# A decoder trunk on one Trainium2 core: where the weight sums of a Strassen-style product are made

## The chip, the cores and the metric

The kernel runs on one core of a Trainium2 chip. The core has five engines with a queue each, worked through in order: TensorE (PE, with PEld for its weight loads), VectorE (DVE), ScalarE (ACT), GpSimd (POOL) and SyncE (SP, which here only starts DMAs). Sixteen DMA engines carry out the transfers that SP and POOL start. An instruction waits on semaphores at the head of its queue, and everything behind it in that queue waits too. The metric is the device time of one execution in microseconds; the kernel before takes 1223.98 us (median of 3 runs, 1222.15 to 1224.19).

## The reference

Two layers over 512 tokens of 1024 features in float32, each a mixer and a squared-ReLU MLP, with RMS norms around both:

```python
for i in range(DEPTH):                       # DEPTH = 2
    h = rms_norm(x, g[0])
    h = mlstm_mixer(h, ...) if i % 2 == 0 else short_conv_mixer(h, ...)
    x = x + rms_norm(h, g[1])
    h = sqrelu_mlp(rms_norm(x, g[2]), w_up[i], w_down[i])   # 1024 -> 4096 -> 1024
    x = x + rms_norm(h, g[3])
```

The order of the stages is thus: mLSTM mixer, first MLP, short convolution, second MLP.

## The kernel before, in words

**Products.** Every float32 product is three matmuls on a high and a low half (`mm3`, L115 to L117). The halves of a weight are made from a loaded raw tile of 128x1024 by `split` (L80 on ScalarE, L81 on VectorE). Raw tiles come from a pool of 7, halves and other large tiles from a pool `u` of 15.

**Quads.** The up projections of both MLPs and the input projection of the convolution are cut into blocks of 1024x512 ("quads"), and each quad is multiplied with seven block products in place of eight (classes `Seven` and `Quad`). With the four 512x256 pieces a, b, c, d of a quad, five factors need sums of pieces: f5 = a+b, f6 = a+b+d, f7 = b+d, f3 = c+f6 (the last is the factor that `run` and `run_first` call f4). A quad without ready sums loads its pieces and adds them on VectorE in `run` (L947, L954, L971, L983). A quad with ready sums (`self.pre`) loads them as they are (`summed`, L902).

**Sums in DRAM.** Twelve quads have ready sums: the first three of the first MLP (`early`), the convolution's six and the first three of the second MLP (`later`). Class `Sums` makes them with DMAs alone: stage 0 copies a, d, b, c from DRAM to four DRAM tiles, started by SyncE (L367); stages 1 to 3 add with accumulating DMAs started by GpSimd (L370): f5 += b and f7 += d, then f6 += f5, then f3 += f6. Each transfer has 512 KB. The stages of `early` stand in the code beside the mixer's `scores_and_core` and output gate, those of `later` beside the loop of the first MLP, but they depend on nothing that is computed.

**The mixer.** Its order is: values for the first two heads (`v_half` 0), gates, eight query and key blocks, values for the other heads (`v_half` 1) with `scores` and `core` in between, eight output gate blocks, then the output projection (`last_product`). GpSimd makes the causal mask for `scores` (L639, `affine_select`), the powers -1/2 in `core` (L743) and those of the norms (L173).

**The first MLP.** `enter` starts the first three quads, then `run_first` and `run` finish quads 0 and 1; then for g = 0 to 5 `down(g)` multiplies with the down weights (two halves `hf` of four token tiles `t`, the sums in `ys` by ScalarE L1053 for g = 0 and VectorE L1055 after) and `run` works on quad g + 2; `fetch_x` (L826, on GpSimd) loads the residual, and `last_product` ends the MLP with gains on GpSimd (L321).

**Order.** A scheduler puts each engine's instructions in order when the program is built; loads and copies from SyncE share one queue, accumulating DMAs and GpSimd's arithmetic another.

Of the kernel before, what the change touches and what calls it, by code (L numbers as in the profile page):

```python
# [8 lines left out]
F32 = mybir.dt.float32  # L9
# [3 lines left out]
ALU = mybir.AluOpType  # L13

P = 128
# [20 lines left out]
AHEAD = 3  # L36
# [3 lines left out]
def tile_hybrid_trunk(  # L40
# [15 lines left out]
    nc = tc.nc  # L56
# [5 lines left out]
    dram = ctx.enter_context(tc.tile_pool(name="dram", bufs=1, space=bass.MemoryType.DRAM))  # L62
# [4 lines left out]
    def pu():  # L67
        return psum("pu", 4)

    def pd():  # L70
        return psum("pd", 2)
# [21 lines left out]
    def raw_tile(shape, dtype=F32):  # L93
        return big.tile([P] + shape, dtype, tag="raw", name="raw", bufs=NRAW)
# [6 lines left out]
    def piece(src, a):  # L101
        return halved(load(src, a), a)
# [6 lines left out]
    def cols_piece(wm, c0):  # L109
        return piece(wm[:, c0 : c0 + P].rearrange("(ko p) m -> p ko m", p=P), KO)  # L110
# [75 lines left out]
    class Plain:  # L186
        def __init__(self):
            self.f = [[unit([4, S], F32R) for _ in range(2)] for _ in range(2)]
# [161 lines left out]
    class Sums:  # L350
# [3 lines left out]
        def __init__(self, wm, c0, c1):  # L354
            def src(kh, c):
                return wm[kh * 512 : (kh + 1) * 512, c : c + 256].rearrange("(p q) m -> q p m", q=P)

            self.a, self.b, self.c, self.d = src(0, c0), src(0, c1), src(1, c0), src(1, c1)
            self.f = [
                dram.tile([P, 4, 256], F32, name=f"f{n}_{len(made)}") for n in (5, 6, 7, 3)  # L360
            ]

        def stage(self, i):
            f5, f6, f7, f3 = self.f
            if i == 0:
                for f, blk in zip(self.f, (self.a, self.d, self.b, self.c)):
                    nc.sync.dma_start(f, blk)  # L367
                return
            for f, blk in (((f5, self.b), (f7, self.d)), ((f6, f5),), ((f3, f6),))[i - 1]:
                nc.gpsimd.dma_start(f, blk, accum_op=ALU.add, max_dma_last_dim=D)  # L370

    made = {}

    def sums_of(key, wm, cols):
        for c in cols:
            made[key, c[0]] = Sums(wm, *c)
        return [made[key, c[0]] for c in cols]
# [82 lines left out]
    later = tc.keep_in_program_order  # L460
# [70 lines left out]
    def rows():  # L531
# [24 lines left out]
    a = T1[0:H, :]  # L556
    nc.vector.scalar_tensor_tensor(
        out=a, in0=thi, scalar=CAP, in1=nb, op0=ALU.mult, op1=ALU.add
# [4 lines left out]
    for c in range(NT):  # L563
# [6 lines left out]
            out=mprev[:, c + 1 : c + 2], in0=M[:, last], in1=nb[:, last], op=ALU.subtract  # L570
        )

    def by_chunk(r):
        return r.rearrange("h (c l) -> h c l", l=P)
# [3 lines left out]
        out=by_chunk(T1[32 : 32 + H, :]),  # L578
        in0=mprev[:, 0:NT].unsqueeze(2).broadcast_to([H, NT, P]),
        in1=M3,  # L580
        op=ALU.subtract,
# [3 lines left out]
        out=by_chunk(T1[96 : 96 + H, :]),  # L585
        in0=by_chunk(a),
        in1=M3[:, :, P - 1 : P].broadcast_to([H, NT, P]),
        op=ALU.subtract,
# [37 lines left out]
    for h in range(H):  # L626
# [4 lines left out]
        for c in range(NT):  # L631
# [8 lines left out]
            out=DT[:, h, :, :],  # L640
# [127 lines left out]
    def take_o(j, o, late):  # L768
        sg = half_kb()
        nc.scalar.activation(sg, o, AF.Sigmoid)  # L770
        put_off(late, lambda: gated(j, sg))
# [12 lines left out]
    def up_cols(gs):  # L784
        return [(g * 512, g * 512 + 256) for g in gs]

    early = sums_of(0, w_up[0], up_cols(range(AHEAD)))
    later = sums_of(
        "conv",
        w_in_conv[0],  # L790
# [3 lines left out]
        + up_cols([1]),  # L794
    ) + sums_of(1, w_up[1], up_cols(range(AHEAD)))

    def all_of(sums, i):
        for sm in sums:
            sm.stage(i)

    def scores_and_core(t):
        if t != 2:
            all_of(early, min(t, 2))
        scores(t)
        if t > 0:
            core(t - 1, 0)

    v_half(1, [piece(v_src(1, i), 2) for i in range(4)], lambda t: None, scores_and_core)
    for j in range(KO):
        w = cols_piece(wi, 2 * QK + D + j * P)  # L810
        o = pu()
        proj_T(o, w, xT, 0, NT)
        take_o(j, o, BLOCK if j < KO - 1 else 0)
        if j == 3:
            all_of(early, 3)
        if j <= NT:
            core((j - 1) % NT, 0 if j == 0 else 1)

# [37 lines left out]
    class Quad:  # L856
# [39 lines left out]
        def put_by(self):  # L896
            self.v = self.values()
            nc.scalar.copy(self.v, by_tile(self.x))

        def summed(self, i):  # L900
            raw = raw_tile([4, 256])
            nc.sync.dma_start(raw, self.pre.f[i])  # L902
            return self.factor(raw)

        def run_first(self):

            tt = nc.vector.tensor_tensor
            f = self.xT.f
            self.claim()
            o, z, y = pd(), pd(), self.y  # L910
            f4, f5, f6, f7 = (self.summed(i) for i in (3, 0, 1, 2))
            f3 = self.factor(self.block(1, 1))
            prod(o, f4, f["a22"], True)
            prod(z, f5, f["p1"], True)
            s5 = self.values()
            nc.scalar.copy(s5, by_tile(z))
            prod(y, f6, f["n2"], False)
            s2 = self.values()
            nc.scalar.copy(s2, by_tile(y))
            prod(z, f3, f["p4"], False)  # L920
            prod(y, f7, f["r3"], False)
            tt(out=s2, in0=by_tile(z), in1=s2, op=ALU.add)
            self.take(1, 0, s2, None)
            s3 = self.values()
            nc.scalar.mul(s3, by_tile(y), -1.0)
            tt(out=s5, in0=by_tile(y), in1=s5, op=ALU.add)
            self.take(1, 1, s5, None)
            self.take(0, 0, self.v, None)
            tt(out=s3, in0=by_tile(o), in1=s3, op=ALU.add)
            self.take(0, 1, s3, None)  # L930
# [56 lines left out]
    def enter(quads):  # L987


        for qd in quads:  # L990
            qd.prepare()
        yield
        for qd in quads:
            qd.prepare_more()
        yield
        flush(2)
        for qd, bank in zip(quads, (pd, pd, pu)):
            qd.begin(bank)
        for qd in quads:
            qd.second()  # L1000
            qd.put_by()
        flush()

    def by_tile(o):
        return o.rearrange("p (u n) -> p u n", u=2)

    def mlp(i, xT, gain_of, tail_of, ends=False, ahead=None):

        NG = FF // P // G
        hs = [None] * (FF // P // 2)  # L1010

        def quad(g):
            def take(nh, half, c, o):
                j = 2 * g + nh
                if o is not None:
                    nc.scalar.activation(c, o, AF.Relu)
                else:
                    o = c
                nc.vector.scalar_tensor_tensor(  # L1019
                    out=c, in0=o, scalar=0.0, in1=c, op0=ALU.max, op1=ALU.mult  # L1020
                )
                if hs[j] is None:
                    hs[j] = pair()
                split(hs[j][:, 0, half], hs[j][:, 1, half], c)

            return Quad(w_up[i], g * 512, g * 512 + 256, xT, take, i)

        ys = []

        def down(g):  # L1030
            if g == 0:
                ys.extend(token_tiles())
            for hf, cs in enumerate(halves()):
                ws = [
                    piece(
                        w_dn[i][r * P : (r + 2) * P, cs].rearrange("(k p) m -> p k m", p=P), 2
                    )
                    for r in (g * G, g * G + 2)
                ]
                for t in range(NT):  # L1040
                    o = pd()
                    for k in range(G):
                        w = ws[k // 2]
                        mm3(
                            o,
                            rows_of(hs, g * G + k, t),
                            (w[:, 0, k % 2, :], w[:, 1, k % 2, :]),
                            k == 0,
                            k == G - 1,
                        )  # L1050
                    yh = ys[t][:, cs]
                    if g == 0:
                        nc.scalar.copy(yh, o)  # L1053
                    else:
                        nc.vector.tensor_tensor(out=yh, in0=yh, in1=o, op=ALU.add)  # L1055

        quads = [quad(g) for g in range(NG)]
        yield from enter(quads[:AHEAD])
        gy, tail = gain_of(), tail_of()
        quads[0].run_first()  # L1060
        quads[1].run(True)
        for g in range(NG - 2):
            if i == 0:
                for k in range(3):
                    if 0 <= g - k < 4:
                        all_of(later[3 * k : 3 * k + 3], g - k)
            down(g)
            quads[g + 2].run(g + 2 < AHEAD)
            if g == NG - 4:
                fetch_x()  # L1070
        last_product(w_dn[i], FF - D, hs[-(KO // 2) :], gy, tail, ys, ends, ahead)
# [111 lines left out]
```

## Time and profile before

| | |
|---|---|
| median of 3 runs | 1223.98 us |
| the profiled execution's own time | 1224.76 us |
| its span, first to last instruction | 1223.1 us |
| TensorE busy in the span | 1090.4 us (89%) |
| VectorE, ScalarE, GpSimd busy | 708.9, 504.1, 121.7 us |
| bytes moved by the DMA queues | 193.52 MB, 158 GB/s |

All times of day below are microseconds from the span's start. Engine names in the profile are PE, PEld, DVE, ACT, POOL, SP; L12 is line 12 of the kernel before. "A <- B" in a wait row says that instructions of line A on the first engine waited for B; the arrow in an instruction's row gives the tile written and the tiles read. The time of an engine's DMA instruction is that of starting the transfer; landing is told apart. A DMA share of 1 means that on average each of the 16 DMA engines had one packet in work; with overlapping packets the share goes above 1.

### The profile page before, as it was taken

What the parts mean: (1) busy time and instruction counts of PE and PEld (TensorE: products, weight loads), DVE (VectorE), ACT (ScalarE), POOL (GpSimd) and SP (SyncE); (2) the same over time, 40 slices, a digit from 0 to 9 for tenths busy, and PEclk for the clock granted to TensorE, in tenths of its full rate; (3) what the DMA queues carried; (4) which work ended last, traced back from release to release, by engine and by line L of the source; (5) the groups of instructions that cost most, each with busy time, mean ns of one, the idle gap of its engine ahead of it and who ended that gap; (6) DMA issues with size and microseconds to landing.
All of it is one profiled execution on the core that took longest, in us unless ns stands there. A gap on an engine that the chain in (4) does not pass through costs nothing. (4 is left out here: it accounts for less than half of the span.)

```text
span 1223.1 us, 16189 instructions
## 1 busy us (share of the span) xinstructions
PE 1090.4 (89%) x6531; PEld 959.8 (78%) x6531; DVE 708.9 (58%) x960; ACT 504.1 (41%) x780; POOL 121.7 (10%) x162
## 2 busy tenths in 40 slices
PE   6898402379999999999999999999999999999997
PEld 4676301267779889889988899998898899899886
DVE  4370101146469566677477687785784765775653
ACT  4341000134357444334335465573565343343331
POOL 2212323210010000000000410001100000000011
PEclk9899655689999999999999999999999999999999
DMA  9999999976227244223416256773373333135111
GB/s 289 268 282 258 244 238 234 215 190 206 93 97 267 79 137 139 69 86 121 153 59 203 86 180 217 247 238 118 103 241 104 104 121 104 60 114 184 64 47 69
DMA packets 146545, 193.52 MB, mean 158 GB/s; under 512 B 7045, under 2 KB 111781, under 8 KB 146470
## 3 DMA queue, kind: packets, MB, share of 16 engines
q1 hardware_dynamic: 116662, 151.07, 39.0%
q0 software_dynamic: 29808, 41.42, 16.5%
q8 instruction: 51, 0.84, 0.3%
q14 instruction: 24, 0.20, 0.1%
HBM read 184.08 MB, written 58.72 MB: 199 GB/s over the span
## 5 line engine op out<-in xcount | busy, mean ns | idle before, releaser
L81 DVE TENSOR_TENSOR u<-raw,u 128x1024 fp32r<-128x1024 f32 (+1 forms) x270 | 320.6, 1202 | 141.5 <-ACT u L80 141.3
L80 ACT CAST u<-raw 128x1024 fp32r<-128x1024 f32 (+1 forms) x270 | 273.7, 1030 | 216.3 <-PE pd L117 160.7
L117 PE MATMUL pu<-u 128*128 128x256 f32 (+1 forms) x1112 | 336.3, 302 | 4.3 <-DVE u L81 4.3
L115 PE MATMUL pu<-u 128*128 128x256 f32 (+1 forms) x1112 | 339.1, 305 | 0.0
L116 PE MATMUL pu<-u 128*128 128x256 f32 (+1 forms) x1112 | 337.6, 304 | 0.8 <-DVE u L81 0.7
L115 PE MATMUL pd<-u,hb 128*128 128x512 f32 (+1 forms) x648 | 254.7, 393 | 0.3 <-DVE t L315 0.2
L116 PE MATMUL pd<-u,hb 128*128 128x512 f32 (+1 forms) x648 | 254.2, 392 | 0.0
L117 PE MATMUL pd<-u,hb 128*128 128x512 f32 (+1 forms) x648 | 254.1, 392 | 0.0
L117 PEld LDWEIGHTS pu<-u 128*128 128x128 f32 x1112 | 211.1, 190 | 13.8 <-DVE u L81 5.4
L116 PEld LDWEIGHTS pu<-u 128*128 128x128 f32 x1112 | 211.2, 190 | 11.3 <-DVE u L81 2.6
L115 PEld LDWEIGHTS pu<-u 128*128 128x128 f32 x1112 | 211.5, 190 | 9.7 <-issue 0.6
L115 PEld LDWEIGHTS pd<-u,hb 128*128 128x128 f32 x648 | 121.8, 188 | 28.9 <-DVE t L315 1.2
L117 PEld LDWEIGHTS pd<-u,hb 128*128 128x128 f32 x648 | 121.7, 188 | 28.0
L116 PEld LDWEIGHTS pd<-u,hb 128*128 128x128 f32 x648 | 121.8, 188 | 27.6 <-DVE u L81 0.6
L115 PE MATMUL pd<-u 128*128 128x256 f32 x312 | 88.9, 285 | 5.2 <-ACT pu L891 3.7
L116 PE MATMUL pd<-u 128*128 128x256 f32 x312 | 88.1, 283 | 0.0
L117 PE MATMUL pd<-u 128*128 128x256 f32 x312 | 87.9, 283 | 0.0
L1055 DVE TENSOR_TENSOR u<-u,pd 128x512 f32<-128x512 f32 x80 | 54.7, 684 | 36.7 <-PE pd L117 36.6
L115 PEld LDWEIGHTS pd<-u 128*128 128x128 f32 x312 | 59.5, 191 | 5.8 <-ACT pu L891 4.1
L181 ACT ACTIVATE junk<-u 128x512 bf16<-128x512 f32 (+1 forms) x49 | 30.6, 624 | 80.1 <-DVE u L318 56.9
L80 ACT CAST hb<-t 128x512 fp32r<-128x512 f32 x80 | 48.9, 621 | 34.8 <-DVE t L1019 27.8
L116 PEld LDWEIGHTS pd<-u 128*128 128x128 f32 x312 | 59.6, 191 | 0.0
(172 smaller groups left out, 878.3 us busy)
## 6 DMA issues: line engine op xcount, KB each, us to landing
raw<-in_w_mlp_down_dram SPq DMA_DIRECT2D x64, 512.0 KB, 4.0
raw<-in_w_mlp_up_dram SPq DMA_DIRECT2D x58, 512.0 KB, 4.5
raw<-f SPq DMA_DIRECT2D x48, 512.0 KB, 4.4
raw<-in_w_in_mlstm_dram SPq DMA_DIRECT2D x24, 512.0 KB, 9.7
f<-in_w_mlp_up_dram SPq DMA_DIRECT2D x24, 512.0 KB, 12.5
f<-f POOLq DMA_DIRECT2D x24, 512.0 KB, 12.1
f<-in_w_in_conv_dram SPq DMA_DIRECT2D x24, 512.0 KB, 18.9
raw<-in_w_in_conv_dram SPq DMA_DIRECT2D x18, 512.0 KB, 4.0
```

Source lines behind the costliest of these rows:

```text
L80: hi = nc.scalar.copy(dst_hi, src)
L81: lo = nc.vector.tensor_tensor(out=dst_lo, in0=src, in1=dst_hi.bitcast(F32), op=ALU.subtract)
L115: nc.tensor.matmul(o, lh, rh, start=first, stop=False, skip_group_check=True)
L116: nc.tensor.matmul(o, lh, rl, start=False, stop=False, skip_group_check=True)
L117: nc.tensor.matmul(o, ll, rh, start=False, stop=last, skip_group_check=True)
L181: nc.scalar.activation(junk(n), src, AF.Square, scale=float(D) ** -0.5, accum_out=ms[:, i : i + 1])
L1055: nc.vector.tensor_tensor(out=yh, in0=yh, in1=o, op=ALU.add)
```

## The change

- The first MLP's quads have no sums in DRAM any more (`early` is gone). Quad 0 loads its four pieces and adds them on VectorE ahead of its run (`Quad.sums`); quads 1 and 2 take the path that later quads of that MLP take already.
- The nine sums of `later` are made by `Sums.make`, called once for each half of `down(g)` in the first MLP until none is left: two for each of g = 0 to 3, one for g = 4. It writes four elements of the token tile t = 3 of `ys` just made (the "mark") into the four DRAM tiles, so that the copies, which overwrite them, wait for it. Mark, four copies and four accumulating DMAs are all started by GpSimd.

```diff
         def __init__(self, wm, c0, c1):
...
-            self.f = [
-                dram.tile([P, 4, 256], F32, name=f"f{n}_{len(made)}") for n in (5, 6, 7, 3)
-            ]
-
-        def stage(self, i):
+            self.all = dram.tile([4, P, 4, 256], F32, name=f"f{len(made)}")
+            self.f = [self.all[i] for i in range(4)]
+
+        def make(self, mark):
             f5, f6, f7, f3 = self.f
-            if i == 0:
-                for f, blk in zip(self.f, (self.a, self.d, self.b, self.c)):
-                    nc.sync.dma_start(f, blk)
-                return
-            for f, blk in (((f5, self.b), (f7, self.d)), ((f6, f5),), ((f3, f6),))[i - 1]:
+            nc.gpsimd.dma_start(self.all[:, 0, 0, 0:1], mark)
+            for f, blk in zip(self.f, (self.a, self.d, self.b, self.c)):
+                nc.gpsimd.dma_start(f, blk)
+            for f, blk in ((f5, self.b), (f7, self.d), (f6, f5), (f3, f6)):
                 nc.gpsimd.dma_start(f, blk, accum_op=ALU.add, max_dma_last_dim=D)
...
-    early = sums_of(0, w_up[0], up_cols(range(AHEAD)))
...
-        if t != 2:
-            all_of(early, min(t, 2))
...
+        def sums(self):
+            tt = nc.vector.tensor_tensor
+            a, b = self.block(0, 0), self.block(0, 1)
+            tt(out=a, in0=a, in1=b, op=ALU.add)
+            d = self.block(1, 1)
+            t2 = raw_tile([4, 256])
+            tt(out=t2, in0=a, in1=d, op=ALU.add)
+            tt(out=b, in0=b, in1=d, op=ALU.add)
+            c = self.block(1, 0)
+            tt(out=c, in0=c, in1=t2, op=ALU.add)
+            self.ts = c, a, t2, b, d
...
-            f4, f5, f6, f7 = (self.summed(i) for i in (3, 0, 1, 2))
-            f3 = self.factor(self.block(1, 1))
+            if self.pre is None:
+                f4, f5, f6, f7, f3 = (self.factor(t) for t in self.ts)
...
+        if quads[0].pre is None:
+            quads[0].sums()
...
+                if i == 0 and later:
+                    later.pop(0).make(yh[0:4, 0:1])
...
-            if i == 0:
-                for k in range(3):
-                    if 0 <= g - k < 4:
-                        all_of(later[3 * k : 3 * k + 3], g - k)
```

The lines of the kernel after differ by 2 or so from those before: L639 becomes L637, L743 becomes L741.

The queue of GpSimd in the mixer, before: the names f5_3 to f3_4 are the DRAM tiles of the convolution's first two quads, hb is the causal mask.

```order
L370 DMA f5_4_725<-in_w_in_conv_dram 512x1x256
L370 DMA f3_3_724<-f6_3_722 512x256
L370 DMA f7_4_727<-in_w_in_conv_dram 512x1x256
L370 DMA f6_4_726<-f5_4_725 512x256
L639 AFFINE_SELECT hb_589<-hb_589 128x512 x2
L370 DMA f5_5_729<-in_w_in_conv_dram 512x1x256
L370 DMA f3_4_728<-f6_4_726 512x256
L370 DMA f7_5_731<-in_w_in_conv_dram 512x1x256
L639 AFFINE_SELECT hb_589<-hb_589 128x512 x2
```

The same place after the change, from the gates' last rows on: small tiles are the operands of the powers.

```order
L616 MEMSET sel_579 36x512
L550 MEMSET u_403 4x4
L637 AFFINE_SELECT hb_589<-hb_589 128x512 x4
L741 TENSOR_TENSOR small_838<-small_838,mhalf_71 128x2
L741 TENSOR_TENSOR small_913<-small_913,mhalf_71 128x2
```

No DMA of the sums stands ahead of mask or powers any more. The queue of SyncE at the output gate's weights (128x8x128) before, where rows of the copies of the second MLP's sums stand around them:

```order
L367 DMA f3_10_752<-in_w_mlp_up_dram 512x1x256
L367 DMA f5_11_753<-in_w_mlp_up_dram 512x1x256
L367 DMA f6_11_754<-in_w_mlp_up_dram 512x1x256
L98 DMA raw_1049<-in_w_in_mlstm_dram 128x8x128
L98 DMA raw_1110<-in_w_in_mlstm_dram 128x8x128
```

and after, with the last value weights (128x2x512) ahead of them:

```order
L98 DMA raw_728<-in_w_in_mlstm_dram 128x2x512
L98 DMA raw_733<-in_w_in_mlstm_dram 128x2x512
L98 DMA raw_989<-in_w_in_mlstm_dram 128x8x128
L98 DMA raw_1050<-in_w_in_mlstm_dram 128x8x128
L98 DMA raw_1111<-in_w_in_mlstm_dram 128x8x128
```

The 37 copies that stood between the last value weights and the first output gate weights are gone from this queue. GpSimd's queue in the first MLP after the change, first two of nine sums (f0 and f1; u_2474 holds the token tile that is marked):

```order
L364 DMA f0_709<-u_2474 4x1
L366 DMA f0_709<-in_w_in_conv_dram 512x1x256 x4
L368 DMA f0_709<-in_w_in_conv_dram 512x1x256 x2
L364 DMA f1_710<-u_2474 4x1
L368 DMA f0_709<-f0_709 512x256
L366 DMA f1_710<-in_w_in_conv_dram 512x1x256 x2
L368 DMA f0_709<-f0_709 512x256
L366 DMA f1_710<-in_w_in_conv_dram 512x1x256 x2
L368 DMA f1_710<-in_w_in_conv_dram 512x1x256 x2
L368 DMA f1_710<-f1_710 512x256 x2
```

Before, GpSimd has nothing in its queue between the gains at the MLP's start and `fetch_x`; now nine sums in such pairs stand there, and `fetch_x` and the last product's gains come behind them. In VectorE's queue, the addition into the marked token tile (L1055 before, L1061 after) of the next g carries a wait on the mark's DMA.

More of the change, by code (lines that the diff above doesn't have):

```diff
@@ L795, in tile_hybrid_trunk @@
     ) + sums_of(1, w_up[1], up_cols(range(AHEAD)))
-    def all_of(sums, i):
-        for sm in sums:
-            sm.stage(i)
     def scores_and_core(t):
-        if t != 2:
-            all_of(early, min(t, 2))
         scores(t)
@@ L813, in tile_hybrid_trunk @@
         take_o(j, o, BLOCK if j < KO - 1 else 0)
-        if j == 3:
-            all_of(early, 3)
         if j <= NT:
@@ L910, in run_first @@
             o, z, y = pd(), pd(), self.y
-            f4, f5, f6, f7 = (self.summed(i) for i in (3, 0, 1, 2))
-            f3 = self.factor(self.block(1, 1))
+            if self.pre is None:
+                f4, f5, f6, f7, f3 = (self.factor(t) for t in self.ts)
+            else:
+                f4, f5, f6, f7 = (self.summed(i) for i in (3, 0, 1, 2))
+                f3 = self.factor(self.block(1, 1))
             prod(o, f4, f["a22"], True)
```

## The prediction, as put on record before the run

> **What bounds the kernel now.** I read the page's 40 slices first.
>
> ```profile
> PE   6898402379999999999999999999999999999997
> ...
> PEclk9899655689999999999999999999999999999999
> DMA  9999999976227244223416256773373333135111
> ```
>
> A slice is 30.6 us. From slice 9 on TensorE is full and sets the time; ahead of that it stands nearly still for five slices while the DMA engines are full. Cut at the stages (first half of the values; the mixer from the third `scores` on; start of the first MLP; its loop up to the convolution), with length, busy time and count of PE, PEld, DVE, ACT and POOL, granted clock, DMA share and GB/s:
>
> ```profile
> 10.38:52.28 41.90, 32.06 (x122) 23.87 (x122) 17.85 (x27) 16.78 (x32) 7.96 (x13) 0.88 1.14 307
> 117.90:365.98 248.08, 142.38 (x625) 115.05 (x625) 82.43 (x177) 64.34 (x132) 49.81 (x54) 0.79 0.84 192
> 365.98:409.09 43.11, 43.11 (x369) 43.11 (x369) 36.92 (x51) 26.51 (x41) 2.24 (x4) 1.00 0.58 208
> 409.09:723.78 314.69, 313.08 (x1906) 277.49 (x1904) 209.88 (x251) 141.48 (x203) 21.87 (x29) 1.00 0.37 119
> ```
>
> Between 117.90 and 365.98, where the first MLP begins, 106 of 248 us are idle. What TensorE waited for up to 366, by the table of waits (total, times, longest), and then what VectorE waited for from 100 to 260:
>
> ```profile
> PE pd L702 <- DVE raw L670: 54.1, 1, 54.1
> PE pd L667 <- DVE raw L670: 22.2, 1, 22.2
> PE pd L709 <- DVE raw L670: 20.0, 1, 20.0
> PE pt L261 <- DVE t L252: 7.2, 3, 3.5
> ...
> PE pu L117 <- DVE u L81: 4.3, 1, 4.3
> ```
>
> ```profile
> DVE small L744 <- POOL small L743: 88.4, 3, 58.2
> DVE raw L670 <- POOL hb L639: 33.5, 1, 33.5
> ```
>
> The three long waits are one story: VectorE's queue stands at a power (L743) or the mask (L639) that GpSimd has not made. GpSimd's timeline says why:
>
> ```profile
> 92.49 1.60 POOL L370 DMA_DIRECT2D f<-in_w_in_conv_dram  x1
> ```
>
> ```profile
> 135.78 1.03 POOL L370 DMA_DIRECT2D f<-f  x1 [10.96 <-DMA f<-f]
> ...
> 137.06 2.19 POOL L639 TENSOR_SCALAR_AFFINE_SELECT hb<-hb 128x512 f32<-128x512 f32 x2
> ```
>
> ```profile
> 251.35 1.03 POOL L370 DMA_DIRECT2D f<-f  x1 [8.07 <-DMA f<-f]
> 252.01 1.11 POOL L743 TENSOR_TENSOR small<-small,mhalf 128x2 f32<-128x2 f32 x1
> ```
>
> Its queue is worked in order, and accumulating DMAs that wait for earlier ones stand ahead of mask and powers. SyncE has a second block, by its own timeline:
>
> ```profile
> 69.45 84.45 SPq L367 DMA_DIRECT2D f<-in_w_in_conv_dram  x24
> 153.94 43.68 SPq L367 DMA_DIRECT2D f<-in_w_mlp_up_dram  x10
> 197.72 21.03 SPq L98 DMA_DIRECT2D raw<-in_w_in_mlstm_dram  x3
> ```
>
> The output gate's weights are not asked for before 197.72, as starting 34 copies took 128 us. Both blocks are made of the sums alone.
>
> **The change part by part.**
>
> *Gone from the mixer.* GpSimd's accumulating DMAs and SyncE's copies; no queue holds anything of the sums before the first MLP. So the three waits go: 54.1 + 22.2 + 20.0 = **96.3 us**. What is late next? VectorE and ScalarE are busy 82 and 64 us in this window, and TensorE's own 142 stays above both, so neither becomes the bound. *The clock* was granted at 0.79 over the window, since TensorE had idled. The groups by shape show the cost:
>
> ```profile
> L115 PE MATMUL pu<-u 128*128 128x512 f32 x80 | 35.0, 438 | 0.0
> L116 PE MATMUL pu<-u 128*128 128x512 f32 x80 | 33.5, 419 | 0.0
> L117 PE MATMUL pu<-u 128*128 128x512 f32 x80 | 32.6, 407 | 0.0
> L115 PE MATMUL pd<-u,hb 128*128 128x512 f32 x64 | 25.6, 400 | 0.2 <-DVE t L315 0.2
> ```
>
> The 240 into `pu` took 38, 19 and 7 ns longer than the 400 ns of the later ones, 5.1 us; the narrower ones stood right behind the waits, and I add almost as much: 9 us (0 to 15). *The other waits* of the window, 106 - 96.3 = 9.7 us, hang partly on loads behind the copies: I take 4 (0 to 9.7). *The first 52 us*: x and the value weights shared the DMA engines (share 1.14) with four copies; there stand the 7.2 and 4.3 us of waits and a clock of 0.88: I take 9 (0 to 14). Together 96.3 + 9 + 4 + 9 = **118.3 us** gained.
>
> *The first MLP's own sums.* Twelve additions more on VectorE. A like one from the loop:
>
> ```profile
> L947 DVE TENSOR_TENSOR raw<-raw 128x1024 f32<-128x1024 f32 x5 | 6.1, 1219 | 0.0
> ```
>
> 12 x 1.22 = 14.6 us. About four fall between 365.98 and 409.09, where VectorE is busy 36.9 of 43.1 us; with 4.9 more it still fits. Four stand in the last product's tail, four in the loop, where VectorE is busy 210 of 315. So their order and not their volume may cost: 2 us (0 to 14.6). If that cover were gone, all 14.6 would show.
>
> *The sums in the first MLP.* I keep the dates of the kernel before and shift later. The loop's dates, from the timelines of ScalarE and VectorE (last token tile of a half, for g = 0, 4 and 5):
>
> ```profile
> 420.99 0.58 ACT L1053 COPY u<-pd 128x512 f32<-128x512 f32 x1
> ```
>
> ```profile
> 584.30 0.68 DVE L1055 TENSOR_TENSOR u<-u,pd 128x512 f32<-128x512 f32 x1
> ```
>
> ```profile
> 626.17 0.68 DVE L1055 TENSOR_TENSOR u<-u,pd 128x512 f32<-128x512 f32 x1
> ```
>
> The first mark may go at 421.6 and the ninth at 585.0; the next addition into that tile, which now waits for the mark, stood at 626.2. Behind it in VectorE's queue stand the factors of the next quads, so a late mark stops TensorE. Eight sums, four pairs, come ahead of the ninth mark in GpSimd's queue; a pair may thus take (626.2 - 421.6) / 4 = **51 us**, and past that every microsecond costs four. By throughput: between 92.49 and 251.35, GpSimd's rows above, the accumulates of nine sums were started in 159 us, with their copies beside them and the engines full, 17.7 us a sum. The share of full engines is 1.18:
>
> ```profile
> 150.00:200.00 50.00, 3.46 (x22) 2.75 (x20) 0.00 (x0) 0.59 (x1) 13.37 (x12) 0.56 1.18 238
> ```
>
> The loop's own loads keep 0.37 of it, so 69% are left, and a pair takes 2 x 17.7 / 0.69 = 51.5 us. By latency, from the accumulating DMAs' landings (median in all, then least, median and greatest of GpSimd's):
>
> ```profile
> f<-f POOLq DMA_DIRECT2D x24, 512.0 KB, 12.1
> ```
>
> ```profile
> DMA to landing us min/median/max: 6.5/13.4/23.5
> ```
>
> In a pair six follow one another (copies, f5, f6, f5, f6 and the mark behind the last f3): at 6.5 us that is 39, less than the loop's own 42 a round, and free; at 12.1 it is 73 and costs 4 x (73 - 51) = 88 us. I take 52, nearest to the throughput: 4 us. `fetch_x` and the last product's gains stand behind the ninth sum, but that is the same lag, not a second one. Weights that land later on shared engines: 2 us (0 to 10), since raw tiles are asked for ahead.
>
> *A rule against the change.* GpSimd started a transfer while VectorE added two tiles:
>
> ```profile
> 368.15 0.53 POOL L835 DMA_DIRECT2D xd<-u  x1 [1.29 <-DVE u L274]
> ```
>
> ```profile
> 367.76 0.69 DVE L238 TENSOR_TENSOR raw<-raw 128x512 f32<-128x512 f32 x1
> ```
>
> The start took 0.53 us beside the addition. The Trainium skill ("DMA: Bandwidth & Descriptors", section "SWDGE vs HWDGE vs iDMA") would issue plain copies from SyncE or ScalarE, since GpSimd writes its descriptors into memory that VectorE's two-port modes lock it out of. By that rule the starts would stretch in the loop, where VectorE is two thirds busy; the row shows none of it.
>
> **Sum.** 118.3 - 2 - 4 - 2 = 110.3 us off the profiled execution's 1224.76 gives 1114.5; the median, 1223.98, is 0.8 us less, so **1114 us**. With every gain at its upper end and no cost: 96.3 + 15 + 9.7 + 14 = 135, 1089. With 9, 4 and 9 at nothing, the costs of 14.6 and 10 in full and a pair of 55 us (16): 1168.
>
> **The rivals.**
>
> 1. *The chain of sums becomes the bound.* A pair takes 55 to 73 us, and VectorE waits at the marked tile, or GpSimd is late at the gains: 16 to 88 us given back, 1126 to 1198. For it: the throughput leaves no slack, and the marks tie the chain to VectorE. Against: the landings were measured with SyncE's 34 copies queued beside them; in the loop stand one pair's transfers and the weights.
> 2. *Starts stretched by VectorE.* Nine starts a sum of 1.03 to 1.6 us; were each twice as long, a pair would grow by some 15 us to 67: 64 given back, 1174. The row above speaks against it.
> 3. *Slower than before.* The same chain at its worst: it decides from a pair of 51 + 114 / 4 = 80 us on, that is landings of 13.3 us in six steps, about the median of 13.4 that the full engines showed. At the greatest, 23.5, a pair takes 141 and the kernel some 1470. Against it speaks what speaks against rival 1.
> 4. *The change doesn't do what it says:* the copies still run early, or something else holds the mixer, as the loads of the output gate. The order of the queues speaks against the first; if half of the three waits came back for the second, 48 us: 1162.
>
> **How the numbers follow.** Forecast (1089 to 1126): 0.62. Rival 1: 0.25. Rival 2: 0.04. Rival 3: 0.03. Rival 4: 0.05; no change at all: 0.01. The range leaves out the tails of the forecast below 1095 and the upper half of rival 1: 1095 to 1160. Faster by over 0.2% (about what a measurement of this kernel can tell from no change) 0.96, within 0.2% 0.01, slower 0.03.
>
> **What would show it.** Right: no wait of L670 or L744 (shifted by two lines) on GpSimd; the clock near 1.0 over the mixer; the first MLP begun near 250; a DMA share near full in its loop and TensorE still full there. Wrong: TensorE idle in the loop behind VectorE's addition into the marked tile, waiting for a DMA; or idle at the convolution's start behind GpSimd's gains; or the start of the first MLP later than 270.

## The result, and the profile after

| kernel | median us | span us | ratio to before, 95% interval |
|---|---|---|---|
| before | 1223.31 (4 runs) | 1223.1 | |
| changed | 1133.72 (1130.37 to 1141.25) | 1134.3 | 0.9277 [0.9226, 0.9327] |

The change is 90 us faster. The range held it; the point, 1114, is 20 us too low. The profiled execution of the changed kernel took 1135.96 us and is the one read here.

The 40 slices of the changed kernel (28.4 us each):

```profile
PE   8999999999999999695989999999999999999997
...
PEclk9999999999999999897999999999999999999999
DMA  8420364145499989898943657733715314316201
```

The nearly empty slices of the mixer (4, 0, 2 and 3 before) are gone. In their place the 17th and the 19th stand at 6 and 5, inside the first MLP, where the DMA engines are nearly full, and the clock falls to 8 and 7 in the same two. What TensorE waited for from 20 us to the first MLP, the two longest rows of the table of waits:

```profile
PE pt L594 <- DVE t L582: 1.5, 1, 1.5
PE pt L775 <- DVE u L745: 0.5, 1, 0.5
```

None of the three waits behind the mask and the powers is left.

To set the stages side by side I date both kernels by the same two products: the first of the first MLP and the one with which the convolution begins. (The prediction's 365.98 is the second kind of product of that MLP; its first is at 361.00.) The first date, of before and then of after:

```profile
361.00 0.37 PE L115 MATMUL pd<-u 128*128 128x256 f32 x1
```

```profile
234.60 0.38 PE L115 MATMUL pd<-u 128*128 128x256 f32 x1 [0.16 <-DVE t L315]
```

The first MLP starts 126.4 us sooner. Of these, 13.0 are won ahead of the mixer's first gate product, which starts at 52.28 before and at 39.32 after. The windows from that product to the first MLP's give the rest, of before and then of after:

```profile
52.28:361.00 308.72, 203.32 (x880) 162.58 (x879) 107.37 (x214) 83.46 (x165) 65.37 (x71) 0.83 0.92 210
```

```profile
39.32:234.60 195.28, 192.95 (x880) 155.14 (x879) 110.19 (x218) 83.48 (x166) 14.49 (x21) 1.00 0.31 98
```

TensorE's idle time falls by 103.1 us there (96.3 of it are the three waits), and the same products take 10.4 us less, at a clock of 1.00 in place of 0.83. Then the windows from the first MLP's start to the convolution and from there to the end, of before:

```profile
361.00:723.78 362.78, 359.31 (x2299) 323.52 (x2297) 250.20 (x307) 171.04 (x251) 24.67 (x34) 1.00 0.39 128
723.78:1223.10 499.32, 490.16 (x3224) 447.07 (x3224) 331.18 (x408) 228.53 (x328) 21.70 (x34) 0.99 0.41 134
```

and of after, with the first MLP cut at its first group and its last product:

```profile
234.60:282.52 47.92, 46.61 (x392) 46.19 (x392) 44.69 (x60) 28.95 (x46) 2.79 (x5) 1.00 0.53 171
282.52:563.30 280.78, 254.32 (x1536) 225.20 (x1537) 168.99 (x191) 106.74 (x136) 74.46 (x85) 0.95 0.93 227
563.30:634.88 71.58, 68.29 (x371) 57.30 (x369) 45.75 (x67) 35.65 (x69) 19.76 (x25) 0.98 0.45 154
634.88:1134.30 499.42, 490.17 (x3224) 447.10 (x3224) 330.95 (x408) 228.43 (x328) 21.68 (x34) 0.99 0.41 135
```

From the convolution on nothing changed (499.3 and 499.4). The first MLP takes 47.92 + 280.78 + 71.58 = 400.3 us where it took 362.8: of the 126.4 us, **37.5 are given back there**. TensorE's busy time is 369.2 us, 9.9 more than before for the same products, at a clock of 0.95 in the loop; the other 27.6 are idle time. What it waited for longest in the first MLP, by the table of waits, and what VectorE waited for at the marked tile:

```profile
PE pd L115 <- DVE u L1061: 26.0, 4, 12.6
PE pd L115 <- ACT hb L80: 1.6, 1, 1.6
```

```profile
DVE u L1061 <- DMA f<-u: 44.5, 5, 13.7
```

Five times VectorE reached the addition into the marked tile (L1061; L1055 before) while GpSimd's mark, a DMA that reads this tile, had not landed; four times TensorE ran dry behind it. The worst place, on VectorE's and then on TensorE's timeline:

```profile
531.82 0.69 DVE L1061 TENSOR_TENSOR u<-u,pd 128x512 f32<-128x512 f32 x1 [13.71 <-DMA f<-u]
```

```profile
532.56 0.79 PE L115 MATMUL pd<-u,hb 128*128 128x512 f32 x1 [12.62 <-DVE u L1061]
```

GpSimd's timeline gives the length of a pair of sums, from the first mark of one to the first of the next (the second mark of each pair, and the first of the fourth at 469.98, are left out here; the rows between show what single steps waited for):

```profile
296.16 0.54 POOL L364 DMA_DIRECT2D f<-u  x1 [48.56 <-ACT u L1059]
...
343.87 1.04 POOL L368 DMA_DIRECT2D f<-f  x1 [4.87 <-DMA f<-in_w_in_conv_dram]
354.11 1.01 POOL L368 DMA_DIRECT2D f<-f  x1 [9.20 <-DMA f<-f]
354.74 0.92 POOL L364 DMA_DIRECT2D f<-u  x1
363.92 2.97 POOL L366 DMA_DIRECT2D f<-in_w_in_conv_dram  x4 [8.26 <-DMA f<-u]
...
414.41 0.92 POOL L364 DMA_DIRECT2D f<-u  x1
...
526.68 0.91 POOL L364 DMA_DIRECT2D f<-u  x1
```

Four pairs take 526.68 - 296.16 = 230.5 us, **57.6 us each**, where TensorE's rounds are 42 and I had allowed 51. By its waits, GpSimd lacked a result only at the first mark; from then on it waited for its own transfers, the marks' own landings among them:

```profile
POOL f L368 <- DMA f<-in_w_in_conv_dram: 65.4, 15, 9.5
POOL f L364 <- ACT u L1059: 48.6, 1, 48.6
POOL f L368 <- DMA f<-f: 46.5, 9, 10.0
...
POOL f L366 <- DMA f<-u: 38.1, 9, 8.3
```

### The profile page after: what moved, and what is told of

Its sections match the earlier page's. It is cut to its first block, busy times and chain, and to the rows that moved or that the text cites. A ratio compares the mean times of both kernels' runs of the same rounds, so it can differ in the third digit from the quotient of the medians.

```text
span 1134.3 us, 16183 instructions
## 1 busy us (share of the span) xinstructions
PE 1086.7 (96%) x6531; PEld 955.7 (84%) x6531; DVE 720.2 (63%) x972; ACT 503.9 (44%) x780; POOL 141.5 (12%) x195
## 5 line engine op out<-in xcount | busy, mean ns | idle before, releaser
L115 PE MATMUL pd<-u,hb 128*128 128x512 f32 (+1 forms) x648 | 258.6, 399 | 28.9 <-DVE u L1061 26.0
L117 PE MATMUL pd<-u,hb 128*128 128x512 f32 (+1 forms) x648 | 256.9, 396 | 1.0 <-DVE hb L81 1.0
L116 PE MATMUL pd<-u,hb 128*128 128x512 f32 (+1 forms) x648 | 256.9, 396 | 0.0
L115 PEld LDWEIGHTS pu<-u 128*128 128x128 f32 x1112 | 210.2, 189 | 10.4 <-ACT u L80 1.3
L115 PEld LDWEIGHTS pd<-u,hb 128*128 128x128 f32 x648 | 123.6, 191 | 60.9 <-DVE u L1061 27.9
L117 PEld LDWEIGHTS pd<-u,hb 128*128 128x128 f32 x648 | 123.5, 191 | 30.0 <-DVE hb L81 1.4
L116 PEld LDWEIGHTS pd<-u,hb 128*128 128x128 f32 x648 | 123.7, 191 | 27.9 <-DVE u L81 0.6
L1061 DVE TENSOR_TENSOR u<-u,pd 128x512 f32<-128x512 f32 x80 | 54.6, 683 | 83.9 <-DMA f<-u 44.5
L115 PEld LDWEIGHTS pd<-u 128*128 128x128 f32 x312 | 59.6, 191 | 4.2 <-ACT pu L880 3.5
L81 DVE TENSOR_TENSOR hb<-t,hb 128x512 fp32r<-128x512 f32 x80 | 54.2, 684 | 9.7 <-ACT hb L80 9.4
```

Source lines behind the costliest of these rows:

```text
L81: lo = nc.vector.tensor_tensor(out=dst_lo, in0=src, in1=dst_hi.bitcast(F32), op=ALU.subtract)
L115: nc.tensor.matmul(o, lh, rh, start=first, stop=False, skip_group_check=True)
L116: nc.tensor.matmul(o, lh, rl, start=False, stop=False, skip_group_check=True)
L117: nc.tensor.matmul(o, ll, rh, start=False, stop=last, skip_group_check=True)
```

## The experiments

Two theories of the 37.5 us. *Coupling:* the chain of sums is longer than TensorE's rounds, and as the mark reads a tile that VectorE must write again, the lag reaches TensorE. *Sharing:* the transfers themselves slow the weights, or VectorE's own sums cost. And of the gain ahead: is it GpSimd's queue, as the prediction said, or SyncE's 128 us of copies? All runs, with the date of the first MLP's first product, its length up to the convolution's, and GpSimd's mean pair:

| run | median us | ratio, 95% interval | first MLP at | its length | pair |
|---|---|---|---|---|---|
| changed | 1133.7 | 0.928 [0.923, 0.933] | 234.6 | 400.3 | 57.6 |
| spare_copies | 1135.7 | 0.927 [0.924, 0.930] | 234.5 | 401.9 | 57.5 |
| early_kept | 1148.6 | 0.938 [0.936, 0.940] | 247.2 | 401.6 | 57.7 |
| early_only | 1184.9 | 0.968 [0.967, 0.970] | 321.2 | 363.0 | |
| mark_apart | 1110.6 | 0.908 [0.905, 0.911] | 234.7 | 373.8 | 55.8 |
| two_at_a_time | 1122.6 | 0.917 [0.916, 0.919] | 234.4 | 387.2 | 53.7 |
| apart_two | 1110.6 | 0.908 [0.906, 0.909] | 234.2 | 377.0 | 53.2 |
| apart_f7_alone | 1108.2 | 0.905 [0.903, 0.907] | 234.4 | 374.3 | 55.1 |
| apart_sooner | 1105.9 | 0.904 [0.902, 0.905] | 234.3 | 370.0 | |
| no_sums | 1107.9 | 0.905 [0.904, 0.907] | 234.9 | 364.6 | |
| six_sums | 1105.8 | 0.904 [0.902, 0.905] | 233.4 | 371.3 | |
| six_marked | 1099.9 | 0.899 [0.898, 0.900] | 234.8 | 367.0 | |
| six_apart | 1098.1 | 0.897 [0.896, 0.899] | 235.1 | 362.0 | |

**Where the gain comes from: SyncE's copies alone.**

```diff
+            if i == 0 and g < 3:
+                for sm in spare[3 * g : 3 * g + 3]:
+                    for f, blk in zip(sm.f, (sm.a, sm.d, sm.b, sm.c)):
+                        nc.sync.dma_start(f, blk)
             down(g)
```

> The changed kernel, and beside it SyncE starts the 36 copies of nine sums where they stood before (their results are not used); GpSimd has nothing of it. By the prediction 96.3 of the front's gain hangs on GpSimd's queue alone, and SyncE's copies cost the late weights and the clock: the first MLP begins 10 to 40 us later than at 234.6, no wait for GpSimd at L668 or L742, 1145 to 1175 us. Rival, SyncE's block is enough to hold the mixer: the first MLP begins at 330 or later, 1230 us or more.

Both expectations missed: no cost of the copies shows (1135.7 and 1133.7, with intervals that overlap). The slices, one window and the longest block of SyncE's starts in this run:

```profile
PE   8999999999999999595989999999999999999997
...
DMA  9997364145499989898943657733715324316201
```

```profile
10.38:52.28 41.90, 41.58 (x177) 32.36 (x178) 24.74 (x41) 24.67 (x43) 5.93 (x13) 1.00 1.06 321
```

```profile
54.77 17.68 SPq L1076 DMA_DIRECT2D f<-in_w_in_conv_dram  x13
72.49 21.75 SPq L1076 DMA_DIRECT2D f<-in_w_mlp_up_dram  x12
```

The copies did run early, as before: the engines are at 1.06 in the first stage, where before they were at 1.14. Yet TensorE is busy 41.58 of these 41.90 us, against 32.06 before, and the first MLP begins at 234.48. So full DMA engines did not hold the first stage, where I had blamed them. On the mixer behind it the run says less: without accumulating DMAs beside them 25 copies were started in 39 us, where before 34 took 128, and the engines are full for three slices, where before they were for eight. The copies alone thus hold nothing up; a block of starts as long as before's is not tried here.

**The first edit alone**: the first MLP's three sums on VectorE, the other nine copied by SyncE and added by GpSimd, unmarked, as before.

```diff
-    early = sums_of(0, w_up[0], up_cols(range(AHEAD)))
...
+        if quads[0].pre is None:
+            quads[0].sums()
```

> Of the three parts only the first: the first MLP's three sums are made by VectorE, the nine later ones stay as before (SyncE copies them, GpSimd adds them, unmarked, so that they run ahead of the mixer). If the length of GpSimd's queue is what held the mixer: three sums of 17.7 us less, 53 us, so the first MLP begins 40 to 55 us sooner than before's 366, at 311 to 326, 1170 to 1190 us. Rival, the first MLP's sums are the block: it begins by 260, 1105 to 1130 us. Other rival, any queue as long as the mixer blocks as much: it begins past 350, 1210 us or more.

The first theory: 1184.9, and the first MLP begins at 321.17, 39.8 us sooner than before's 361.00 (the expectation's 366 is the other date). GpSimd's queue is shorter by three sums; its last accumulating DMA ahead of the powers goes at 196.68, where before it went at 251.35:

```profile
196.68 1.01 POOL L369 DMA_DIRECT2D f<-f  x1 [8.34 <-DMA f<-f]
197.33 1.12 POOL L742 TENSOR_TENSOR small<-small,mhalf 128x2 f32<-128x2 f32 x1
```

That is 54.7 us for three sums, the 53 that 17.7 a sum foretold. Not all of it reaches the first MLP: behind this power TensorE still had 120.4 us of products to do, where before it had 100.4. The run also settles VectorE's own sums in the first MLP:

```profile
321.17:684.18 363.01, 359.79 (x2296) 323.53 (x2296) 259.70 (x316) 170.81 (x249) 24.62 (x34) 1.00 0.39 125
```

363.0 us with them and 362.8 without: they are hidden (VectorE is busy 259.7 of 363).

**The other edit alone**: nine marked sums, the first MLP's three in DRAM as before.

```diff
+    early = sums_of(0, w_up[0], up_cols(range(AHEAD)))
...
+        if t != 2:
+            for sm in early:
+                sm.stage(min(t, 2))
```

> Of the three parts only the marked one: the nine later sums as in the changed kernel, the first MLP's three sums in DRAM as before (SyncE's 12 copies, GpSimd's 12 accumulating DMAs ahead of the mixer), none of them on VectorE. If it is the length of GpSimd's blocked queue (nine sums' accumulations behind one another): three sums are through before the powers are wanted, the first MLP begins within 20 us of 234.6, 1130 to 1155 us. Rival, the first sums alone block the mixer: a wait for GpSimd of 40 us or more is left, 1175 to 1225.

As expected: 1148.6 us, the first MLP begins 12.6 us later than in the changed kernel. All of that is lost in the first stage. The first gate product of the mixer, in this run and in the changed kernel:

```profile
52.29 1.09 PE L501 MATMUL pd<-u,raw 128*128 128x512 f32 x4
```

```profile
39.32 0.85 PE L492 MATMUL pd<-u,raw 128*128 128x512 f32 x3
```

With spare_copies beside it (39.17) it is three sums' accumulating DMAs in GpSimd's queue, ahead of the powers of the first norm, that cost these 13 us: up to 56 us VectorE waits 13.0 us for these powers, and 2.7 in the changed kernel.

**The mark apart.** VectorE (ScalarE for the first group) copies one element of the result to a tile of its own, and the mark reads that.

```diff
-                    later.pop(0).make(yh[0:4, 0:1])
+                    m = mk[:, len(later) : len(later) + 1]
+                    (nc.scalar.copy if g == 0 else nc.vector.tensor_copy)(m, yh[0:4, 0:1])
+                    later.pop(0).make(m)
```

> The mark is read from a tile of its own (one element copied from each result), which nobody overwrites; the sums and their order on GpSimd stay. Coupling theory (VectorE's addition at L1061 has to wait until the mark has been read, and TensorE stands behind it): VectorE's 44.5 us of waits for a DMA there and TensorE's 26.0 us go, the clock comes back, 1095 to 1110 us, with pairs still at 55 to 60 us, since nothing makes the chain shorter. Rival, the DMA engines are shared (late weights) or VectorE has too much to do: TensorE's waits move to the raw tiles or to the factors, 1122 to 1136. Third: the chain is then late for its readers or for GpSimd's own gains at the last product: waits there, and no gain.

The coupling is shown: the pair is nearly as long as before, 55.8 us ((519.71 - 296.52) / 4), all waits at this addition are gone, and 26.5 of the 37.5 us come back. The time misses the range by 0.6 us, since the waits of the third expectation came too, though not its "no gain". What TensorE and VectorE still waited for, and where:

```profile
PE pt L261 <- DVE t L252: 6.7, 1, 6.7
```

```profile
561.35 0.75 DVE L274 SCALAR_TENSOR_TENSOR u<-u,small 128x512 f32<-128x512 f32 x1 [12.10 <-POOL small L173]
```

GpSimd is now late for its power at the last product: the ninth sum stands ahead of it. It is the fault of the kernel before, in small.

**How long is a pair, and why?** First two sums together (one mark each on the first half's result, then eight copies, four additions, two, two); then the same with the mark apart; then, with the mark apart, f7's addition left out, so that f7 holds a single block.

```diff
+                    two = [later.pop(0) for _ in later[:2]]
+                    for sm in two:
+                        sm.make(yh[0:4, 0:1])
+                    for n in range(3):
+                        for sm in two:
+                            sm.add(n)
```

> Two sums are begun together under one result of the first half of a group, so that each dependent step carries two sums: three dependent steps a pair in place of six. Latency theory (the chain's length is the number of dependent steps times a landing of some 8 us): a pair's own work shrinks to 35 to 42 us, marks follow TensorE's rounds of 42 us, the waits at L1061 go, 1095 to 1112 us. Throughput theory (the engines can't move more beside the weights): the marks stay 55 us or more apart, 1125 to 1140.

> The mark apart and two sums at a time, to measure a pair free of VectorE's wait: three dependent steps with two sums each. If the number of steps alone sets a pair (apart_f7_alone: one transfer of eight left out, still 55.1 us): 35 to 45 us, so marks at TensorE's round of 42, GpSimd's power in time, 1098 to 1106 us. If a step's landing grows with what is under way in it, the engines being full: a pair of 48 to 55 us, GpSimd's power late by 5 us or more as in mark_apart, 1106 to 1113 us.

```diff
-            for f, blk in ((f5, self.b), (f7, self.d), (f6, f5), (f3, f6)):
+            for f, blk in ((f5, self.b), (f6, f5), (f3, f6)):
```

> The mark apart, and one of each sum's four additions (f7) left out, so that f7 holds a single block: seven transfers a sum in place of eight, and the chain of dependent steps as long as before, as nothing but the reader waits for f7. Throughput theory: a pair drops from 55.8 us by about 2 x 3.2 us (512 packets of 101 ns over 16 engines) to 48 to 51, GpSimd's power at the last product comes in time, 1098 to 1106 us. Latency theory: a pair stays at 54 to 57 us, 1107 to 1113 us.

Halving the dependent steps took 2.6 us from a pair (55.8 to 53.2), leaving out one transfer of eight 0.7. two_at_a_time, at 1122.6, fell between its two ranges: 14.4 of TensorE's 26.0 us behind the addition were left. apart_f7_alone came out by its latency theory, apart_two by its second theory in pair and time. Landings of mark_apart, and then of apart_two, between the first mark and the ninth, median us from issue:

```profile
f<-in_w_in_conv_dram POOLq DMA_DIRECT2D x36, 512.0 KB, 8.8
...
f<-f POOLq DMA_DIRECT2D x16, 512.0 KB, 8.5
...
f<-mk POOLq DMA_DIRECT2D x9, 0.0 KB, 7.8
```

```profile
f<-in_w_in_conv_dram POOLq DMA_DIRECT2D x36, 512.0 KB, 12.7
...
f<-f POOLq DMA_DIRECT2D x16, 512.0 KB, 11.0
```

With twice as much under way a step lands later, which eats most of what fewer steps save. So neither my throughput (which leaving out a transfer should have moved by 6 us) nor the count of steps alone sets the pair. How the two combine stays open. two_at_a_time, with the coupling still in it, gained 11 us; the marks apart, one sum or two at a time made no difference (1110.6 both). In apart_two GpSimd's power was in time, against the expectation (VectorE's longest wait for it was 1.7 us). There TensorE stood 4.2 and 5.1 us (the second time by way of VectorE) behind ScalarE, which waited for weights of the convolution, from 520 to 565 us:

```profile
ACT u L80 <- DMA raw<-in_w_in_conv_dram: 7.3, 3, 3.8
```

**Removing the second lag.** Beginning two sums under the first MLP's first product:

```diff
             qd.put_by()
+            if qd is quads[0] and qd.pre is None and later:
+                m = const.tile([4, 1], F32, tag="mk0", name="mk", bufs=1)
+                nc.scalar.copy(m, qd.x[0:4, 0:1])
+                for _ in range(2):
+                    later.pop(0).make(m)
```

> The mark apart, and the first two sums begun under a result of the first MLP's first product, some 30 us before the first group's result. In mark_apart GpSimd's first power at the last product was 12.1 us late behind the ninth sum, and TensorE idled 6.7 us for it with the clock then down. If that lag is what is left: GpSimd is through 25 to 35 us sooner, the wait goes, 1097 to 1105 us. Rival, the engines' throughput: the sums collide with the first quads' blocks and the weights, TensorE waits for raw tiles or factors at the start of the loop, 1107 us or more.

Between the two expectations, 1105.9: the late power is gone, but TensorE now loses 5.5 us at the loop's start. six_sums, the same with the second MLP's three sums given to VectorE, has that loss too, and shows it:

> The mark apart, begun under the first MLP's first product, and only the convolution's six sums in DRAM; VectorE makes the second MLP's three as it does the first's. By the results so far VectorE's own sums of three quads cost an MLP nothing (early_only: 363.0 us from the first MLP's first product to the convolution's, before 362.8), and the chain of sums cost the first MLP 6.9 us in apart_sooner (369.7). With three sums fewer the chain ends by about 430, far ahead of the last product: the first MLP takes 363 to 367 us, the convolution and the second MLP 499 to 502, 1098 to 1104 us. Rival, the second MLP has no room for VectorE's additions (no_sums lost some 6 us from the convolution on): 1105 to 1110 us.

```profile
285.33 1.22 DVE L951 TENSOR_TENSOR raw<-raw 128x1024 f32<-128x1024 f32 x1 [6.40 <-DMA raw<-in_w_mlp_up_dram]
```

```profile
287.81 0.80 PE L115 MATMUL pd<-u,hb 128*128 128x512 f32 x1 [6.73 <-DVE t L982]
```

The number is the rival's, its mechanism isn't: from the convolution on this run takes 498.3 us, so VectorE's sums for the second MLP are free; a late weight tile in the first MLP costs. So sharing does show, here, in apart_sooner and in apart_two, beside the coupling. And without any sum in DRAM:

```diff
-                if i == 0 and later:
-                    later.pop(0).make(yh[0:4, 0:1])
```

> No sum in DRAM at all: VectorE makes them for every quad, 36 additions more in the convolution and the second MLP, 44 us by 1.22 us each. If the chain of sums is all that the first MLP lost: it takes 350 to 362 us from its first product to the convolution's, as before the change (357.8), in place of 400.3; and, should VectorE hide its additions (it was busy 331 of 500 us there), the convolution and the second MLP take 500 and the whole 1088 to 1100 us. Rival, VectorE's own sums cost the first MLP as well: 370 us or more there. If the additions aren't hidden, up to 44 us more from the convolution on, to 1140 us.

```profile
234.89:599.44 364.55, 359.79 (x2297) 323.74 (x2297) 264.03 (x320) 171.91 (x250) 24.90 (x34) 1.00 0.38 122
599.44:1105.60 506.16, 491.29 (x3226) 446.76 (x3224) 364.84 (x440) 227.37 (x327) 22.59 (x34) 0.99 0.37 119
```

The expected 350 to 362 was missed by 2.6 (it was drawn around 357.8, counted from the other kind of product; the like figure of before is 362.8), and the total by 8, since 6.7 us are lost from the convolution on; still this kernel is 26 us faster than the changed one. In the changed form the sums in DRAM cost more than they save. They pay when their chain is short, six sums in place of nine:

```diff
-    ) + sums_of(1, w_up[1], up_cols(range(AHEAD)))
+    )
```

> The changed kernel with the second MLP's three sums left to VectorE, and the mark still in the tile of results. If the loss is a lag that grows (pairs of some 57 us against rounds of 42): six sums end with the fourth mark pair not needed, so only the first of the waits at L1061 is left (TensorE stood 2.2 us at 420 in the changed kernel, and 10.8 and 12.6 at the seventh and ninth marks, which are gone): 1098 to 1108 us. If every mark costs its wait: two thirds of the 26 us remain, 1115 to 1125 us.

> six_sums without its early beginning: the first sum is marked from the first group's result, as in the changed kernel; the mark apart, and the second MLP's three sums on VectorE. In six_sums TensorE lost 6.7 us at 287.8 behind VectorE's addition, which stood 6.4 us for a raw tile of w_mlp_up while the early sums filled the engines; in mark_apart, without the early beginning, that wait was not there, and the ninth sum held GpSimd's power for 12.1 us instead. If these two were what was left: both are gone, the first MLP takes 362 to 367 us (before 362.8), the rest 498 to 500, 1096 to 1102 us. Rival, something else in the first MLP pays for the transfers whatever their place: 368 us or more there, 1103 to 1108 us.

Both as expected. six_marked (the line above alone) lost 2.0 us at L1061:

```profile
PE pd L115 <- DVE u L1061: 2.0, 1, 2.0
```

six_apart (with the mark apart) lost none there. Its windows of the first MLP and of the rest:

```profile
235.08:597.08 362.00, 359.74 (x2296) 323.41 (x2297) 259.96 (x320) 171.11 (x251) 72.92 (x88) 1.00 0.71 194
597.08:1095.60 498.52, 489.20 (x3225) 445.52 (x3224) 343.98 (x420) 228.63 (x328) 22.56 (x34) 1.00 0.41 132
```

Nothing of the 37.5 us is left (362.0, before 362.8), with six sums still running beside the weights. At **1098.1 us** six_apart beats both kernels, by 10.3% and by some 3%. The intervals of six_marked and six_apart overlap, so with six sums no gain from the mark apart is shown in the whole time.

## Why the prediction was right, and where its size was off

- *Three waits of 96.3 us on GpSimd's queue go*: right, and shown. No wait of the mixer is longer than 1.5 us, and early_only moves the first MLP with the length of that queue.
- *First 52 us, 9*: measured 13.0 (52.28 to 39.32). The size was near, the reason wrong. I blamed x and value weights sharing the engines with the copies; spare_copies has the copies and loses nothing, early_kept has the accumulating DMAs and loses it all. *Clock 9 and other waits 4*: together with the 96.3 they were to give 109.3, and 126.4 - 13.0 = 113.4 came: 10.4 by the clock and 103.1 - 96.3 = 6.8 by other waits. Copies alone cost neither, by spare_copies; how much of the 6.8 hung on loads behind the long block of before stays open.
- *VectorE's own sums, 2*: 0.2 by early_only.
- *Later weights, 2*: 2.6 in the changed kernel. ScalarE stood 3.5 us for a raw tile of the convolution, and TensorE 1.6 and 1.0 us behind it:

```profile
569.83 1.05 ACT L80 CAST u<-raw 128x1024 fp32r<-128x1024 f32 x1 [3.50 <-DMA raw<-in_w_in_conv_dram]
```

- *The chain of sums, 4*: this is the term that was mis-sized. It measured some 35, the 37.5 less the late weights. The formula gives the date of the addition behind the ninth mark, and there it held in the main. This addition came at 531.82, which is 32.0 us later than before's 626.17 less the 126.4 gained. Four pairs of 57.6 us in place of 51 make 26 of that; the first mark was 1.0 late, and the ninth mark's own landing, which the formula left out, took the other 5.1 (526.68 to 531.82). That TensorE's waits there are 26.0 as well proves less, since the 32.0 hold slower products too. The pair was put at 52 by the throughput, while the latency beside it gave 39 to 73; by apart_two and apart_f7_alone neither sets it alone. Its count of six steps has one landing of a mark, while GpSimd waited for both marks of a pair, 38.1 us for nine; how much of a pair that cost no run shows. And behind the ninth mark the clock was still down, 0.90 up to 563.30. From 531.82 to the convolution the products took 3.0 us longer than before, which the term left out though I had counted the clock in the mixer.
- *GpSimd's gains are the same lag, not a second one*: right while TensorE was held back itself. With the mark apart they are a second one, of 12.1 us for VectorE and 6.7 for TensorE.
- *Rival 1*, with its 1126 to 1198, is what happened, at its mild end, and the first sign of being wrong that the prediction names came: TensorE idle in the loop behind the addition into the marked tile. What spoke for it, that the throughput leaves no slack, was weighed too lightly. The forecast's own span, 1089 to 1126, misses 1133.72; the range holds it because it took in the lower half of this rival. Luck is in it as well: the gain was put 8.1 us too low (118.3 where 126.4 came), and this hid part of costs that were put 29.5 us too low (8 where 37.5 came).
- *Rival 2*, starts stretched by VectorE, is refuted for these starts. (Its 15 us was too small besides: 18 starts of 1.03 us are 18.5.) Accumulating starts by line, of before (read with the engines full) and of after:

```profile
L370 POOL DMA_DIRECT2D f<-f x24 | 26.3, 1097 | 145.3 <-DMA f<-f 72.2 <-DMA f<-in_w_in_conv_dram 38.8 <-DMA f<-in_w_mlp_up_dram 29.5
```

```profile
L368 POOL DMA_DIRECT2D f<-f x18 | 18.8, 1045 | 88.4 <-DMA f<-f 46.5 <-DMA f<-in_w_in_conv_dram 26.6 <-DMA f<-in_w_mlp_up_dram 12.2
```

1045 ns beside a VectorE that is busy 169 of 281 us, 1097 before. The Trainium skill's advice in "DMA: Bandwidth & Descriptors", section "SWDGE vs HWDGE vs iDMA", is to keep plain copies off GpSimd. By spare_copies following it could have been free, but no run moves the marked copies to SyncE. Its reason does not show in this trace, and is not tested by it either, since no run shows VectorE in one of the two-port modes.

By the steps as measured: 1224.76 - 126.4 + 37.5 = 1135.9, the profiled execution's 1135.96.

## What to carry to other kernels

A DMA that reads a tile which compute will write again is a wait for that compute; if the DMA's queue can fall behind, read from a copy that nobody rewrites. When a chain of dependent transfers is laid beside a loop, compare its length with the loop's round at the landings under load, and count each queue's own compute behind it: in the kernel before and in mark_apart it was GpSimd's small operations behind waiting DMAs that stopped TensorE, while late loads cost TensorE less than 10 us in the runs with the sums beside the first MLP. And measure the plain alternative: making the sums on the idle share of VectorE beat the marked chain by 26 us.

## What the runs showed of the hardware that was not expected

- Sixteen bytes took as long as 512 KB: in mark_apart, between the first mark and the ninth, the marks landed after 7.8 us in the median, the accumulated half megabytes after 8.5. A mark is a full step of the chain; nine of them held GpSimd 38.1 us in the changed kernel.
- 18.9 MB of copies that nobody waits for cost nothing beside the mixer (spare_copies, DMA share 1.06 in the first stage), while in the kernel before, which had accumulating transfers beside them and ahead of GpSimd's compute, the first MLP began 126 us later. With those transfers beside them 34 copies took SyncE 128 us to start, without them 25 took 39 us.
